# Feed-forward norm weights: from the normalised token rows to the rows of the first feed-forward weights

## The chip, the cores and the metric

One core of a Trainium2 chip. The metric is the device time of one execution of the whole program in microseconds, as the median of several runs. Everything is float32 in and out. The engines are TensorE (PE, with its weight loads as PEld), VectorE (DVE), ScalarE (ACT), GpSimd (POOL), and SyncE (SP), which here only issues transfers. Each engine works through its own list of instructions in order.

## The reference, cut to what matters

A transformer-like block on 1024 tokens of width 1024: two mixing branches, a cross-attention into 256 memory tokens, then a gated feed-forward layer. The part that the change touches is the norm ahead of the feed-forward layer and that layer's first product.

```python
def rms_norm(x, gain):
    y = x * lax.rsqrt(jnp.mean(x * x, axis=-1, keepdims=True) + RMS_EPS)
    return y * gain
...
h = h + memory_cross_attention(rms_norm(h, norm_mem_q), rms_norm(mem, norm_mem_kv), ...)
f_a, f_b = jnp.split(rms_norm(h, norm_ffn) @ w_ffn_in, 2, axis=-1)    # 1024 x 5632
h = h + (jax.nn.silu(f_a) * f_b) @ w_ffn_out
```

`norm_ffn` has one weight for each of the 1024 channels of a token. Since those channels are the inner dimension of the first product, (r · h · diag(g)) @ W equals (r · h) @ (diag(g) · W): the weight may be multiplied into a column of the tokens or into a row of W.

## The kernel before

**Products.** Each float32 matrix product is made from halves: a value is split into a rounded part (hi, written by ScalarE: `split`, "CAST" in the rows) and the rest (lo, a subtraction on VectorE), and three matmuls add hi·hi, hi·lo and lo·hi. On top of that the big products use a seven-product scheme (Strassen's kind) over 2 x 2 blocks. So the weights go through sums and differences before they are split, and the tokens do too (`A11`, `A12`, `S1` to `S4` and `A22` are the seven token operands, each in hi and lo).

**Normalised tokens.** `norm_blocks(t)` handles one tile of 128 tokens, t = 0 to 7, woven between the last rows of the cross-attention (`mem_out`). It takes the root of the mean square (`rstd`: squares on ScalarE into `ss`, a power on GpSimd into `r`, a refinement on VectorE), forms the normalised rows `xs` (in `norm_scale`, one VectorE instruction that multiplies by the root and by a row `gbc` of weights), transposes `xs` on TensorE and builds the token operands. The row of weights comes from `bcast_gain`, a transfer that repeats the 1024 weights on all 128 partitions.

**The first feed-forward weights.** There are 22 hidden tiles of 128 columns (`NF`). For tile j two blocks of 1024 rows x 128 columns are fetched, `raw` (the a half) and `rawb` (the b half), each as 128 partitions x 8 row blocks x 128 columns, 512 KB. `w_first` splits raw into `whi` and `wlo`. `w_sums` makes sums inside raw and rawb on VectorE and splits three of them. `w_last` splits what is left into `wdh` and `wdl`; its second split is the last reader of raw. Tiles 0 and 1 take another way: `ahead` fetches them much earlier as `wpr`, during the gated linear units of the mixing stage, and parks all split operands in a scratch tensor (`w_d`).

**The loop over hidden tiles**, from tile 2 on:

```python
for j in range(2, NF):
    start(j); end(j - 1); w_last(j); middle(j)
    if j + 1 < NF:
        w_first(j + 1); w_sums(j + 1)
    f = w_fetch(j + 2) if j + 2 < NF else f
    if j % 2: out_fetch(j // 2, f.ins)
    else:     gated(j // 2 - 1)
```

`start` runs products 1 and 2 of tile j and copies them out (`a`), `end` runs products 3 and 4 of tile j - 1 and makes the gated result `g` (GpSimd multiplies its second half, a · c), `middle` runs products 6, 7 and 5 (copied out as `a` and `c`). For every second tile `gated` builds four sums of two gated tiles and stores them (`c_d`), and for every other one `out_fetch` loads two row blocks of the second feed-forward weights (`wo`), whose sums `out_sums` puts into `t_d`.

**What sets the order.** A scheduler orders each engine's list and adds the semaphores; tiles come from pools. `raw` has two buffers for all tiles, `rawb` shares five buffers (tag "tmp") with `g` and others, and a transfer into a buffer goes out when the last reader of its former tile is done. PSUM banks are named `mm` (three), `sc` (two), `pv` (two) and `misc`. All fetches of weights stand in SP's one list.

**Around it.** During the cross-attention GpSimd multiplies the attention weights by one over their sum (`pe <- pe,sm`, a column spread over a row), during the gated linear units it multiplies by gates (`sg <- sg,ga`), and earlier, in the mixing attention, it makes low halves (`pl <- pf,ph`). In the second feed-forward product blocks `or` are fetched and split into `oh` and `ol`.

The functions that the change touches, and what calls them:

Of the kernel before, what the change touches and what calls it, by code (L numbers as in the profile page):

```python
# [9 lines left out]
F32 = mybir.dt.float32  # L10
# [3 lines left out]
AF = mybir.ActivationFunctionType  # L14
ALU = mybir.AluOpType
# [4 lines left out]
P = 128  # L20
# [46 lines left out]
def f32(ap):  # L67
    return ap.bitcast(F32)
# [53 lines left out]
class Shared:  # L122
# [5 lines left out]
    def tmp(self, name, dt=F32):  # L128
        return self.pool.tile([P, D], dt, tag="tmp", bufs=5, name=name)
# [15 lines left out]
class Block:  # L145
# [25 lines left out]
    def behind(self, ins):  # L171
        return nullcontext() if ins is None else self.tc.issue_after(ins.ins)

    def wload(self, pieces, cols, pool_lo=False, behind=None, into=None):

        raw = self.wpool.tile([P, RAW], F32, tag="raw", bufs=2, name="raw")
        for off, shape, src in pieces:
            n = shape[0] * shape[1]
            self.S.dma_start(raw[:, off:off + n].rearrange("p (k c) -> p k c", k=shape[0]), src)
        hi, lo = into or [self.wpool.tile([P, WSLOT], F32R, tag=t_, name=t_) for t_ in ("whi", "wlo")]  # L180
        with self.behind(behind):
            self.split(hi[:, :cols], lo[:, :cols], raw[:, :cols], pool_lo)
        return hi, lo

    def wblock(self, w, k0, nk, c0, nc_, pool_lo=False, behind=None):

        src = w[k0 * P:(k0 + nk) * P, c0:c0 + nc_].rearrange("(k p) c -> p k c", p=P)
        hi, lo = self.wload([(0, (nk, nc_), src)], nk * nc_, pool_lo, behind)
        return tuple(t[:, :nk * nc_].rearrange("p (k c) -> p k c", k=nk) for t in (hi, lo))

    def product(self, ps, l, r, start, stop, a=None, **kw):
# [142 lines left out]
def hybrid_block_kernel(ctx: ExitStack, tc: tile.TileContext, x, mem, norm_mix, w_in, b_forget,  # L334
# [36 lines left out]
    with tc.tile_pool(name="st2", bufs=1, reuse_waits="tile") as s2:  # L371
        stage_tail(B, big, s2, sh, x, glu, aT, gate_d, kv_d, sums_d, w_fox_o, w_mix_out, norm_mem_q[0], w_mem_q,
                   w_mem_o, norm_ffn[0], w_ffn_in, w_ffn_out, norm_final, out)
# [226 lines left out]
def stage_tail(B, big, s2, sh, x, glu, aT, gate_d, kv_d, sums_d, w_fox_o, w_mix_out, g_mq, w_mem_q, w_mem_o, g_ffn,  # L600
               w_ffn_in, w_ffn_out, g_fin, out):
    nc, V, A, G, T, S, small, ident = B.nc, B.V, B.A, B.G, B.T, B.S, B.small, B.ident
    NS2 = 16

    def bslot(dt=F32, name="b"):
        return big.tile([P, D], dt, tag="big", name=name)

    def slot(dt=F32, name="t"):
        return s2.tile([P, D], dt, tag="t", bufs=NS2, name=name)
# [6 lines left out]
        return t_  # L616


    am_d = B.dram.tile([4, P, D], F32, name="am_d")
    s3_d = B.dram.tile([2, P, D], F32, name="s3_d")  # L620
    fox, part, xm, mixw, msets = {}, {}, {}, {}, []
# [78 lines left out]
    def ahead(j, mk):  # L700

        def keep(n, t_):
            A.dma_start(w_d[j, n], f32(t_))

        def pair(n):
            hl = mk("wph", F32R), mk("wpl", F32R)
            return hl, [[t_[:, o:o + 512] for t_ in hl] for o in (0, 512)]

        def fetch():
            pre[j] = [mk("wpr") for _ in range(2)]  # L710
            for r_, c in zip(pre[j], (0, FH)):
                S.dma_start(r_.rearrange("p (k c) -> p k c", k=8),
                            w_ffn_in[:, c + j * P:c + (j + 1) * P].rearrange("(k p) c -> p k c", p=P))

        def plain():
            hl, _ = pair(0)
            B.split(*hl, pre[j][0])
            for i, t_ in enumerate(hl):
                keep(i, t_)

        def sums():
            ra, rb = pre[j]
            b22 = rb[:, 512:]
            hl, (w5, w6) = pair(2)
            V.tensor_add(ra[:, 512:], ra[:, 512:], b22)
            V.tensor_add(ra[:, :512], ra[:, :512], rb[:, :512])
            V.tensor_add(rb[:, :512], rb[:, :512], b22)
            B.split(*w5, ra[:, :512])
            V.tensor_add(ra[:, 512:], ra[:, 512:], ra[:, :512])
            V.tensor_add(ra[:, :512], ra[:, :512], b22)  # L730
            B.split(*w6, ra[:, :512])
            for i, t_ in enumerate(hl):
                keep(2 + i, t_)

        def seventh():
            e_ = mk("wph", F32R)
            B.split(e_[:, :512], e_[:, 512:], pre[j][1][:, :512])
            keep(4, e_)

        def rest():  # L740
            ra, rb = pre.pop(j)
            hl, (w3, w4) = pair(5)
            B.split(*w3, rb[:, 512:])
            B.split(*w4, ra[:, 512:])
            for i, t_ in enumerate(hl):
                keep(5 + i, t_)

        return [fetch, plain, sums, seventh, rest]

    ahead0, ahead1 = ahead(0, lambda name, dt=F32: slot(dt, name)), ahead(1, tmp)  # L750
    for j in range(8):
        if j > 3:
# [26 lines left out]
    H = [bslot(name=f"h{t}") for t in range(NT)]  # L779
# [52 lines left out]

    weave([lambda h=h: mem_q(h, 0) for h in range(MH)], [lambda t=t: turned(t, ("misc", "pv")) for t in range(4, 8)])
    kth, ktl, vh, vl = [slot(F32R, "kv") for _ in range(4)]
    gf = B.bcast_gain(s2, g_ffn)
    sc = float(DH * 2) ** -0.5
    pts, oT, pes = {}, {}, {}

# [90 lines left out]
    def put(name, mk, i, src, neg=False):  # L929

        hi_, lo_ = blocks(name, mk)
        for kk in range(2):
            sv = src[:, kk * 256:(kk + 1) * 256].rearrange("p (k c) -> p k c", k=2)
            hi, lo = [a[kk][:, :, i * P:(i + 1) * P] for a in (hi_, lo_)]
            if neg:
                A.activation(hi, sv, AF.Copy, scale=-1.0)
                V.scalar_tensor_tensor(out=lo, in0=sv, scalar=-1.0, in1=f32(hi), op0=ALU.mult, op1=ALU.subtract)
            else:
                B.split(hi, lo, sv)

    def norm_blocks(t):
        i = t % 4
        xs = s2.tile([P, D], F32, tag="xs", bufs=1, name="xs")
        B.norm_scale(xs, H[t], B.rstd(H[t]), gf)
        S.dma_start(h_d[t], H[t])
        ps = [B.turn(xs, b, ("misc", "pv")[b]) for b in range(2)]
        if t < 4:
            for b in range(2):
                xf = sh.half("xf")
                A.copy(xf, ps[b])  # L950
                S.dma_start(x_d[i][:, 512 * b:512 * b + 512], xf)
                put(("A11", "A12")[b], slot, i, xf)
            return
        xa, sx, s3 = tmp("xa"), tmp("sx"), sh.half("s3")
        S.dma_start(xa, x_d[i])
        a11, a12, s1n, a22 = xa[:, :512], xa[:, 512:], sx[:, :512], sx[:, 512:]
        A.copy(a22, ps[1])
        V.tensor_sub(s3, a11, ps[0])
        V.tensor_sub(s1n, ps[0], a22)
        V.tensor_sub(a11, s1n, a11)  # L960
        V.scalar_tensor_tensor(out=a12, in0=a11, scalar=-1.0, in1=a12, op0=ALU.mult, op1=ALU.subtract)
        put("S2", slot, i, a11)
        put("S3", bslot, i, s3)
        put("S1", bslot, i, s1n, neg=True)
        S.dma_start(r_d[i][:, :512], a12)
        S.dma_start(r_d[i][:, 512:], a22)
# [9 lines left out]
    def w_fetch(j):  # L976
        raws[j] = B.wpool.tile([P, RAW], F32, tag="raw", bufs=2, name="raw")[:, :D], tmp("rawb")
        for r_, c in zip(raws[j], (0, FH)):
            f = S.dma_start(r_.rearrange("p (k c) -> p k c", k=8),
                            w_ffn_in[:, c + j * P:c + (j + 1) * P].rearrange("(k p) c -> p k c", p=P))  # L980
        return f

    def wpair(j):
# [136 lines left out]
    for t in range(4):  # L1120
        mem_out(t)
        if t:
            norm_blocks(t - 1)
        for f in late[4 * t:4 * t + 4 if t < 3 else None]:
            f()
    norm_blocks(3)
    w_first(0)
    w_first(1)
    for t in range(4, 8):
        mem_out(t)  # L1130
        if t > 4:
            norm_blocks(t - 1)
    w_sums(0)
    start(0)
    norm_blocks(7)
    start(1)
    w_fetch(2)
    w_last(0)
    w_sums(1)
# [6 lines left out]
    middle(1)  # L1146
    w_sums(2)
    out_fetch(0, w_fetch(3).ins)
    for j in range(2, NF):
        start(j)  # L1150
        end(j - 1)
        w_last(j)
        middle(j)
        if j + 1 < NF:
            w_first(j + 1)
            w_sums(j + 1)
        f = w_fetch(j + 2) if j + 2 < NF else f
        if j % 2:
            out_fetch(j // 2, f.ins)
        else:  # L1160
            gated(j // 2 - 1)
# [66 lines left out]
    for m, (n, p) in enumerate(seq):  # L1228
# [6 lines left out]
        if n < 3 and p in (2, 4, 6, 8):  # L1235
            t = 4 * (n - 1) + p // 2 - 1
# [802 lines left out]
```

## Time and profile before

| | us |
|---|---|
| median of 3 runs (lowest, highest) | 1493.9 (1493.74, 1496.89) |
| the profiled execution, its time | 1489.17 |
| its span, first to last instruction | 1487.5 |
| PE busy | 1447.5 (97%) |
| DVE busy | 1026.5 (69%) |
| ACT busy | 681.6 (46%) |
| POOL busy | 274.2 (18%) |
| mean granted TensorE clock | 0.998 |

Times inside the span count from its first instruction. The cross-attention with the norms lies at about 717 to 910 us, the loop over the first feed-forward weights from there to about 1285 us, the second feed-forward product and the last norm behind it; the gated linear units of the mixing stage, with the `wpr` fetches, lie at about 530 to 715 us.

How its rows read. A group row has a source line, the engine, the operation, output and inputs by the program's names, how often, busy time, the mean of one in ns, and the idle time of the engine just ahead with what ended it. A timeline row has the start, the duration, the engine, line and operation, and in brackets how long the engine had waited and for whom. A row of waits names who waited, for whom, how many us in all, how often, and the longest. SPq is the queue of SyncE, its rows are transfers issued. A duration can hold time in which the instruction stood on its engine without working.

### The profile page before, as it was taken

The numbers are of one execution on the slowest core, as the hardware profiler recorded it, in microseconds if no ns is written. First come the engines' busy times: TensorE is split into PE (matmuls) and PEld (weight loads), VectorE is DVE, ScalarE is ACT, GpSimd is POOL, SyncE is SP. The second block draws the span as 40 slices with busy tenths as digits, with TensorE's granted clock in tenths as the row PEclk, the third lists the DMA queues.
The fourth block names the chain that finished last, engine by engine and source line by source line (L and its number), as shares of the span: only waits on it lengthen the run. The fifth ranks groups of instructions, "written<-read, shape, count | busy, mean of one in ns | idle before, by whom it ended". The sixth has DMA issues, their size and how long they took to land.

```text
span 1487.5 us, 20506 instructions
## 1 busy us (share of the span) xinstructions
PE 1447.5 (97%) x7271; PEld 1248.2 (84%) x7271; DVE 1026.5 (69%) x1841; ACT 681.6 (46%) x1215; POOL 274.2 (18%) x359
## 2 busy tenths in 40 slices
PE   8999999999999999999999999999999999999997
PEld 7889888988777678788888778888888888888886
DVE  7678544555777857689766787777777776576555
ACT  6423333423667764444545654333333333354443
POOL 1036675200112114210102200000000000101001
PEclk9999999999999999999999999999999999999999
DMA  9565668642132476778431376555555554897553
GB/s 303 129 152 117 194 183 151 189 136 35 16 63 54 114 214 204 240 248 316 151 100 57 142 256 233 163 163 163 170 169 166 169 167 159 300 391 256 200 169 114
DMA packets 202249, 257.14 MB, mean 173 GB/s; under 512 B 36041, under 2 KB 127081, under 8 KB 201634
## 3 DMA queue, kind: packets, MB, share of 16 engines
q1 hardware_dynamic: 194946, 239.05, 53.2%
q10 hardware_dynamic: 7200, 16.78, 3.0%
q8 instruction: 57, 0.93, 0.3%
q14 instruction: 46, 0.38, 0.1%
HBM read 175.56 MB, written 83.20 MB: 174 GB/s over the span
## 4 chain that ended last, share of the span: by engine, by line
PE 80%; DVE 8%; DMA 4%; ACT 4%; issue 3%; POOL 1%; SPq 0%; POOLq 0%; DVEq 0%; ACTq 0%
PE mm L196 37%; PE sc L196 16%; PE pv L196 16%; PE mm L142 3%; PE misc L196 2%; PE mm L194 1%; DMA raw<-in_w_mem_kv_dram 1%; DMA or<-in_w_ffn_out_dram 1%; DVE junk L1803 1%; PE sc L194 1%; ACT pf L1835 1%; DVE wlo L213 1%; DVE xs L255 1%; DVE hb L1774 1%; POOL r L231 1%
## 5 line engine op out<-in xcount | busy, mean ns | idle before, releaser
L213 DVE TENSOR_TENSOR wlo<-raw,whi 128x1024 fp32r<-128x1024 f32 (+2 forms) x119 | 128.4, 1082 | 86.8 <-ACT whi L212 83.9
L212 ACT CAST whi<-raw 128x1024 fp32r<-128x1024 f32 (+2 forms) x119 | 107.4, 903 | 131.5 <-DVE raw L1015 29.0
L213 DVE TENSOR_TENSOR ol<-or,oh 128x1024 fp32r<-128x1024 f32 x73 | 92.0, 1266 | 62.2 <-ACT oh L212 61.1
L212 ACT CAST oh<-or 128x1024 fp32r<-128x1024 f32 x73 | 76.4, 1048 | 94.8 <-PE pv L196 30.6
L196 PE MATMUL mm<-uh,whi 128*128 128x512 f32 x280 | 107.6, 384 | 0.1
L196 PE MATMUL mm<-uh,wlo 128*128 128x512 f32 x280 | 106.5, 381 | 0.2 <-DVE wlo L213 0.2
L196 PE MATMUL mm<-ul,whi 128*128 128x512 f32 x280 | 106.3, 380 | 0.0
L1076 POOL TENSOR_TENSOR g<-a,c 128x512 f32<-128x512 f32 x22 | 35.3, 1607 | 363.4 <-ACT a L1075 344.8
L231 POOL TENSOR_TENSOR r<-ms,mhalf 128x1 f32<-128x1 f32 (+1 forms) x30 | 20.5, 686 | 320.0 <-DVE ms L227 252.0
L1838 POOL TENSOR_TENSOR pl<-pf,ph 128x512 fp32r<-128x512 f32 (+1 forms) x32 | 37.3, 1166 | 224.2 <-DVE ph L1837 224.2
L1835 ACT ACTIVATE pf<-sc 128x512 f32<-128x512 f32 (+1 forms) x96 | 46.8, 490 | 35.0 <-DVE sc L1831 21.3
L196 PEld LDWEIGHTS mm<-uh,wlo 128*128 128x128 f32 x280 | 52.9, 189 | 8.4 <-DVE wlo L213 1.3
L196 PEld LDWEIGHTS mm<-uh,whi 128*128 128x128 f32 x280 | 53.1, 190 | 6.3 <-DVE mc L1803 0.4
L196 PEld LDWEIGHTS mm<-ul,whi 128*128 128x128 f32 x280 | 53.1, 190 | 6.0
L196 PE MATMUL pv<-S3h,we 128*128 128x512 f32 x176 | 56.4, 380 | 0.2 <-ACT S3h L212 0.2
L1841 DVE TENSOR_TENSOR pl<-pf,ph 128x512 fp32r<-128x512 f32 (+2 forms) x64 | 34.9, 550 | 17.8 <-ACT ph L1840 17.2
L196 PE MATMUL mm<-yh,whi 128*128 128x512 f32 x104 | 39.5, 383 | 3.9 <-ACT sg L1287 3.4
L1300 POOL TENSOR_TENSOR sg<-sg,ga 128x512 f32<-128x512 f32 x16 | 29.1, 1840 | 72.3 <-DVE sg L1293 27.6
L196 PE MATMUL mm<-oh,ol 128*128 128x512 f32 x106 | 40.2, 379 | 0.0
L196 PE MATMUL mm<-oh 128*128 128x512 f32 x106 | 40.2, 379 | 0.0
L196 PE MATMUL mm<-ol,oh 128*128 128x512 f32 x106 | 40.2, 379 | 0.0
L196 PE MATMUL sc<-uh,whi 128*128 128x512 f32 x104 | 39.8, 383 | 0.0
(722 smaller groups left out, 4609.2 us busy)
## 6 DMA issues: line engine op xcount, KB each, us to landing
or<-c_d SPq DMA_DIRECT2D x77, 256.0 KB
wo<-in_w_ffn_out_dram SPq DMA_DIRECT2D x22, 512.0 KB
c_d<-g SPq DMA_DIRECT2D x44, 256.0 KB
t_d<-wo SPq DMA_DIRECT2D x44, 256.0 KB
or<-t_d SPq DMA_DIRECT2D x44, 256.0 KB
raw<-in_w_ffn_in_dram SPq DMA_DIRECT2D x20, 512.0 KB
rawb<-in_w_ffn_in_dram SPq DMA_DIRECT2D x20, 512.0 KB
raw<-in_w_in_dram SPq DMA_DIRECT2D x18, 512.0 KB
```

What stands on the lines that cost most here:

```text
L142: return lambda *a, **k: self.tc.keep_in_program_order(op(*a, **k))
L194: return self.T.matmul(ps, l, r, start=start, stop=stop)
L196: self.T.matmul(woven(ps, a).rearrange(order), l, halves(r, a).rearrange(order), start=start, stop=stop, **kw)
L212: self.copied = self.A.copy(hi, src)
L213: self.lowered = (self.G if pool_lo else self.V).tensor_sub(lo, src, f32(hi))
L231: self.G.tensor_tensor(out=r, in0=v, in1=self.mhalf[:, 0:n], op=ALU.pow)
L255: self.V.scalar_tensor_tensor(out=xs, in0=src, scalar=r, in1=gb, op0=ALU.mult, op1=ALU.mult)
L1076: G.tensor_mul(g[:, 512:], a1, c1)
L1300: self.B.G.tensor_mul(self.out[j][:, cs], self.out[j][:, cs], ga)
L1835: self.exp = A.activation(halves(pf[:, off:], 64), woven(ps[:, off:], 64), AF.Exp)
L1838: G.tensor_sub(pl[:, off:], pf[:, off:], f32(ph[:, off:]))
L1841: V.tensor_sub(pl[:, off:], pf[:, off:], f32(ph[:, off:]))
```

## The change

It does three things. A new transfer at the program's start loads the 1024 weights as eight columns of 128 (`gain_columns`, tile `gf`), so that row p of row block k finds its weight on its own partition. `row_gain`, one GpSimd instruction over 128 x 1024, multiplies a fetched block of first weights by those columns, in place; it stands behind each fetch of `raw`, `rawb` and `wpr`, 44 times in all. And `norm_blocks` scales the tokens by their root alone, with one ScalarE activation in place of VectorE's instruction. The row of weights `gbc` is not loaded any more.

```diff
+    def gain_columns(self, g, name):
+        gc = self.const.tile([P, 8], F32, name=name)
+        self.S.dma_start(gc, g.rearrange("(k p) -> p k", p=P))
+        return gc
+
+    def row_gain(self, w, gc):
+        wv = w.rearrange("p (k c) -> p k c", k=8)
+        self.G.tensor_tensor(out=wv, in0=wv, in1=gc.unsqueeze(2).to_broadcast([P, 8, wv.shape[-1]]), op=ALU.mult)
...
+    gf = B.gain_columns(g_ffn, "gf")
     am_d = B.dram.tile([4, P, D], F32, name="am_d")
...
             for r_, c in zip(pre[j], (0, FH)):
                 S.dma_start(r_.rearrange("p (k c) -> p k c", k=8),
                             w_ffn_in[:, c + j * P:c + (j + 1) * P].rearrange("(k p) c -> p k c", p=P))
+                B.row_gain(r_, gf)
...
-    gf = B.bcast_gain(s2, g_ffn)
...
         xs = s2.tile([P, D], F32, tag="xs", bufs=1, name="xs")
-        B.norm_scale(xs, H[t], B.rstd(H[t]), gf)
+        A.activation(xs, H[t], AF.Copy, scale=B.rstd(H[t]))
         S.dma_start(h_d[t], H[t])
...
             f = S.dma_start(r_.rearrange("p (k c) -> p k c", k=8),
                             w_ffn_in[:, c + j * P:c + (j + 1) * P].rearrange("(k p) c -> p k c", p=P))
+            B.row_gain(r_, gf)
         return f
```

`wload` and `wblock` also get a parameter `gain` that no caller sets. Lines of the changed file lie 10 to 13 further down than those of before (L1076 is now L1089, L858 is L870, L212 is L223).

**Three places in the order of instructions.** GpSimd's list at the start of the loop, before (`r` is the root of a norm, `g` the gated half):

```order
L231 TENSOR_TENSOR r_8944<-ms_8943,mhalf 128x1
L231 TENSOR_TENSOR r_9027<-ms_9026,mhalf 128x1
L1076 TENSOR_TENSOR g<-a_9174,c_9200 128x512
L1076 TENSOR_TENSOR g<-a_9253,c_9279 128x512
L1076 TENSOR_TENSOR g<-a_9386,c_9412 128x512
```

The same place after:

```order
L242 TENSOR_TENSOR r_9031<-ms_9030,mhalf 128x1
L181 TENSOR_TENSOR rawb<-rawb,gf 128x1024 x2
L1089 TENSOR_TENSOR g<-a_9180,c_9206 128x512
L181 TENSOR_TENSOR rawb<-rawb,gf 128x1024
L1089 TENSOR_TENSOR g<-a_9259,c_9285 128x512
L181 TENSOR_TENSOR raw<-raw,gf 128x1024
L181 TENSOR_TENSOR rawb<-rawb,gf 128x1024
L1089 TENSOR_TENSOR g<-a_9394,c_9420 128x512
```

Between two products g of the loop now stand one product of raw and one of rawb; g itself waits behind them in GpSimd's list.

GpSimd's list in the cross-attention, before:

```order
L231 TENSOR_TENSOR r_7578<-ms_7577,mhalf 128x1
L858 TENSOR_TENSOR pe<-pe,sm 128x512 x11
L231 TENSOR_TENSOR r_8315<-ms_8314,mhalf 128x1
L231 TENSOR_TENSOR r_8439<-ms_8438,mhalf 128x1
L858 TENSOR_TENSOR pe<-pe,sm 128x512 x2
```

And after:

```order
L870 TENSOR_TENSOR pe<-pe,sm 128x512 x5
L181 TENSOR_TENSOR raw<-raw,gf 128x1024
L870 TENSOR_TENSOR pe<-pe,sm 128x512 x2
L181 TENSOR_TENSOR raw<-raw,gf 128x1024
L870 TENSOR_TENSOR pe<-pe,sm 128x512 x4
L242 TENSOR_TENSOR r_8319<-ms_8318,mhalf 128x1
```

The products of the first two raw tiles (2 and 3) stand in the midst of the attention weights' products.

VectorE's list at the norm of the last token tile, before:

```order
L237 TENSOR_TENSOR rt_9028<-r_9027 128x1
L238 SCALAR_TENSOR_TENSOR rt_9028<-rt_9028,ms_9026 128x1
L239 SCALAR_TENSOR_TENSOR r_9027<-rt_9028,r_9027 128x1
L255 SCALAR_TENSOR_TENSOR xs<-h_6956,r_9027,gbc 128x1024
L958 TENSOR_TENSOR s_9048<-xa,misc 128x512
```

After, VectorE's list, where the row of xs is gone:

```order
L248 TENSOR_TENSOR rt_9032<-r_9031 128x1
L249 SCALAR_TENSOR_TENSOR rt_9032<-rt_9032,ms_9030 128x1
L250 SCALAR_TENSOR_TENSOR r_9031<-rt_9032,r_9031 128x1
L970 TENSOR_TENSOR s_9052<-xa,misc 128x512
L1064 TENSOR_TENSOR a_9010<-a_9010,sc 128x512
```

And ScalarE's list after, where it has come in:

```order
L223 CAST S2h<-xa 128x2x128 x2
L1065 ACT_TABLE_LOAD
L1065 ACTIVATE a_9010<-a_9010 128x512
L956 ACTIVATE xs<-h_6960,r_9031 128x1024
L223 CAST whi<-raw 128x1024
L1062 COPY a_9087<-mm 128x512
```

The scaling stands behind a Silu of `start(0)` and ahead of the cast of a raw tile and the copy of a bank.

More of the change, by code (lines that the diff above doesn't have):

```diff
@@ L172, in behind, with wload @@
         return nullcontext() if ins is None else self.tc.issue_after(ins.ins)
-    def wload(self, pieces, cols, pool_lo=False, behind=None, into=None):
+    def gain_columns(self, g, name):
[5 more added lines that the diff above has]
+        self.G.tensor_tensor(out=wv, in0=wv, in1=gc.unsqueeze(2).to_broadcast([P, 8, wv.shape[-1]]), op=ALU.mult)
+    def wload(self, pieces, cols, pool_lo=False, behind=None, into=None, gain=None):
         raw = self.wpool.tile([P, RAW], F32, tag="raw", bufs=2, name="raw")
@@ L180, in wload @@
         hi, lo = into or [self.wpool.tile([P, WSLOT], F32R, tag=t_, name=t_) for t_ in ("whi", "wlo")]
+        if gain is not None:
+            self.row_gain(raw[:, :cols], gain)
         with self.behind(behind):
@@ L183, in wload, with wblock @@
         return hi, lo
-    def wblock(self, w, k0, nk, c0, nc_, pool_lo=False, behind=None):
+    def wblock(self, w, k0, nk, c0, nc_, pool_lo=False, behind=None, gain=None):
         src = w[k0 * P:(k0 + nk) * P, c0:c0 + nc_].rearrange("(k p) c -> p k c", p=P)
-        hi, lo = self.wload([(0, (nk, nc_), src)], nk * nc_, pool_lo, behind)
+        hi, lo = self.wload([(0, (nk, nc_), src)], nk * nc_, pool_lo, behind, gain=gain)
         return tuple(t[:, :nk * nc_].rearrange("p (k c) -> p k c", k=nk) for t in (hi, lo))
```

## The prediction

> **What bounds the kernel now.** I read the page first: its span and section 1.
>
> ```profile
> span 1487.5 us, 20506 instructions
> PE 1447.5 (97%) x7271; PEld 1248.2 (84%) x7271; DVE 1026.5 (69%) x1841; ACT 681.6 (46%) x1215; POOL 274.2 (18%) x359
> ```
>
> TensorE bounds it: it idles for 40 us in all, and GpSimd (POOL) looks free. But a share says nothing of a stage, so next come the stretches with the changed work: cross-attention with the norms (800 to 910 us), and the loop over the first feed-forward weights. Each row of this table has a stretch, its length, and then what PE, PEld, DVE, ACT and POOL are busy in it.
>
> ```profile
> 800.00:910.00 110.00, 103.32 (x538) 86.12 (x537) 87.11 (x199) 64.04 (x178) 15.34 (x18) 1.00 0.54 192
> 910.00:1255.00 345.00, 345.00 (x1600) 302.11 (x1600) 256.81 (x361) 132.00 (x210) 31.55 (x20) 1.00 0.51 164
> ```
>
> In the loop TensorE never idles, and its clock is full (1.00). What could make it idle is seen from the waits of the engines that feed it.
>
> ```profile
> DVE wlo L213 <- ACT whi L212: 51.0, 24, 3.2
> DVE wdl L213 <- PE pv L196: 14.1, 11, 1.7
> DVE g L1071 <- PE mm L196: 7.8, 8, 1.1
> ACT whi L212 <- DMA raw<-in_w_ffn_in_dram: 25.3, 11, 3.4
> ```
>
> VectorE (DVE) waits longest for a cast on ScalarE (ACT), and that waits for the weight's transfer. So I followed one raw tile through two tiles of the loop, in timelines by engine.
>
> ```profile
> 1001.76 1.22 DVE L213 TENSOR_TENSOR wlo<-raw,whi 128x1024 fp32r<-128x1024 f32 x1 [2.77 <-ACT whi L212]
> 1014.21 0.68 DVE L213 TENSOR_TENSOR wdl<-raw,wdh 128x512 fp32r<-128x512 f32 x1
> 1014.43 1.60 POOL L1076 TENSOR_TENSOR g<-a,c 128x512 f32<-128x512 f32 x1 [16.60 <-ACT a L1075]
> 1014.81 1.77 DVE L1115 TENSOR_TENSOR wo<-wo 128x512 f32<-128x512 f32 x1
> 1014.92 0.38 SPq L979 DMA_DIRECT2D raw<-in_w_ffn_in_dram  x1
> 1018.88 1.04 ACT L212 CAST whi<-raw 128x1024 fp32r<-128x1024 f32 x1
> 1019.96 1.23 DVE L213 TENSOR_TENSOR wlo<-raw,whi 128x1024 fp32r<-128x1024 f32 x1 [2.78 <-ACT whi L212]
> 1020.32 0.59 ACT L1063 COPY c<-mm 128x512 f32<-128x512 f32 x1 [0.39 <-PE mm L196]
> 1028.09 0.69 DVE L1071 SCALAR_TENSOR_TENSOR g<-mm,a 128x512 f32<-128x512 f32 x1 [1.07 <-PE mm L196]
> 1030.46 0.69 DVE L213 TENSOR_TENSOR wdl<-rawb,wdh 128x512 fp32r<-128x512 f32 x1 [1.69 <-PE pv L196]
> 1032.27 0.68 DVE L213 TENSOR_TENSOR wdl<-raw,wdh 128x512 fp32r<-128x512 f32 x1
> 1033.03 0.38 SPq L979 DMA_DIRECT2D raw<-in_w_ffn_in_dram  x1
> 1037.93 1.22 DVE L213 TENSOR_TENSOR wlo<-raw,whi 128x1024 fp32r<-128x1024 f32 x1 [2.69 <-ACT whi L212]
> ```
>
> This is a ring. The last subtraction that reads a raw tile (wdl<-raw, ends 1014.89) frees one of two raw buffers; the fetch goes out at 1014.92; the cast follows at 1018.88; wlo at 1019.96; VectorE, in order, works to the next wdl<-raw (ends 1032.95); then the next fetch. Its four legs: 1001.76 to 1014.89, 13.1 us, with the four sums of `gated`; 5.1 to 1019.96; 13.0 to 1032.95, of which 1.07 + 1.69 = 2.8 us are waits for TensorE; 5.0 to 1037.93. Without those waits the ring needs 33.4 us for two tiles, and TensorE takes 36.2. So the ring is slack by 2.8 us, no more.
>
> A second thing stands there. POOL's product begins at 1014.43 and VectorE's 128x512 addition takes 1.77 us instead of 0.68: it is held until POOL ends (1016.03). The other way, a VectorE operation that reads PSUM is not held while POOL works:
>
> ```profile
> 607.88 2.50 POOL L1300 TENSOR_TENSOR sg<-sg,ga 128x512 f32<-128x512 f32 x2 [10.44 <-DMA ga<-gate_d]
> 609.76 0.69 DVE L647 TENSOR_TENSOR gb<-gb,pv 128x512 f32<-128x512 f32 x1 [3.84 <-DMA gb<-gate_d]
> ```
>
> **The change, part by part.** *44 products of 128x1024 on POOL.* The trace has no such size; the nearest rows are half of it.
>
> ```profile
> L858 POOL TENSOR_TENSOR pe<-pe,sm 128x512 f32<-128x512 f32 x16 | 16.6, 1040 | 60.1 <-DVE sm L856 59.8
> L1838 POOL TENSOR_TENSOR pl<-pf,ph 128x512 fp32r<-128x512 f32 x24 | 30.6, 1276 | 69.3 <-DVE ph L1837 69.3
> L1076 POOL TENSOR_TENSOR g<-a,c 128x512 f32<-128x512 f32 x22 | 35.3, 1607 | 363.4 <-ACT a L1075 344.8
> ```
>
> The first also spreads a column over a row, as the new product does: 2 x 1.04 = 2.1 us, which I take. Twice the second, 2.55, and twice the third (which holds waits behind VectorE), 3.2, are the upper ends. By the Trainium skill's GPSIMD Engine Reference, section 3.1, a float32 tensor_tensor of 2048 elements takes 4497 ns on this engine; half of it is an estimate of 2.25 us, and the sum below would rise from 34 to about 39 us with it. No run here shows that size yet.
>
> *In the loop* the product of raw stands between the landing and the cast: twice 2.1 per two tiles on the two short legs. 33.4 + 4.2 = 37.6 us, 1.4 over TensorE's 36.2. The products of rawb hold VectorE while it works on the long legs:
>
> ```profile
> 1008.35 0.39 SPq L979 DMA_DIRECT2D rawb<-in_w_ffn_in_dram  x1
> 1019.90 0.43 SPq L979 DMA_DIRECT2D rawb<-in_w_ffn_in_dram  x1
> ```
>
> The first comes 6.6 us after its leg begins and needs four to land, so it is multiplied before that leg's wdl<-raw; the second comes behind the two wo fetches of the leg before and lands within the next leg. Each holds 2.1 less one PSUM operation of 0.6 that passes: 1.5. Together 40.6, so 4.4 us more than TensorE needs. Low end: no hold, 1.4. High end: 2.55 instead of 2.1 in all four (1.8), nothing passes (1.2), and POOL's g comes before wdl<-raw instead of behind it (1.1): 8.5.
>
> The Trainium skill (SBUF — State Buffer, "Who interferes with whom") says that a VectorE instruction with two SBUF inputs and a GpSimd instruction that reads SBUF exclude each other for a whole instruction, and one with a single SBUF input is free. The 1.77 and the 0.69 us above agree; by a shared bandwidth instead, the ring would take the 37.6 us.
>
> How TensorE is reached: the copy c (1020.32, 0.59 us) is queued on ScalarE behind the raw cast, and the third product into that bank needs it, at this row of the chain:
>
> ```profile
> 1025.46 2.59 PE mm L196 x12
> ```
>
> The cast ends at 1019.92 and could end at 1025.46 - 0.59 = 1024.87: a head start of 4.9 us. Raw fetches run every 18.1 us from 924.24 to 1232.69:
>
> ```profile
> 924.24 0.38 SPq L979 DMA_DIRECT2D raw<-in_w_ffn_in_dram  x1
> 1232.69 0.38 SPq L979 DMA_DIRECT2D raw<-in_w_ffn_in_dram  x1
> ```
>
> That is 17 intervals, 8.5 pairs: 8.5 x 4.4 - 4.9 = 32.5 us (low 8.5 x 1.4 - 4.9 = 7, high 8.5 x 8.5 - 4.9 = 67).
>
> *Eight normalisations move from DVE to ACT.* What TensorE waits for them is small, whatever DVE saves:
>
> ```profile
> PE misc L261 <- DVE xs L255: 2.7, 4, 1.5
> L255 DVE SCALAR_TENSOR_TENSOR xs<-h,r,gbc x16: 1275/1284/1287, 717.4 to 886.2; 128x1024 f32<-128x1024 f32 x16
> ```
>
> On ACT one costs about the 1.04 us of the 128x1024 cast, in a stage where ACT is busy for 64 of 110 us. I take a gain of 2.5; the ends are 0 and all idle time of that stage, 110 - 103.3 = 6.7.
>
> *Two products in the cross-attention* stand in POOL's queue ahead of pe products, and POOL waits there for the raw tile:
>
> ```profile
> 804.10 0.38 SPq L979 DMA_DIRECT2D raw<-in_w_ffn_in_dram  x1
> ```
>
> Landing 3.9 us later like those of the loop, it lets the next pe, and TensorE's transposes of it, come up to 1.5 us late: 1.0 taken, 0 to 1.5. The first two rawb products delay the sums of tile 2: 1.0 taken, 0 to 2.
>
> *Four wpr products.* For the first two VectorE has no gap, and TensorE already stalls at the end of that stretch:
>
> ```profile
> 582.79 4.07 POOL L1300 TENSOR_TENSOR sg<-sg,ga 128x512 f32<-128x512 f32 x2 [1.04 <-DVE sg L1293]
> 585.69 1.71 DVE L725 TENSOR_TENSOR wpr<-wpr 128x512 f32<-128x512 f32 x1
> 612.88 0.48 PE L196 MATMUL mm<-yh,whi 128*128 128x512 f32 x1 [3.42 <-ACT sg L1287]
> ```
>
> Two holds of 2.1 are 4.2 us; I take 2.5 at that stall, 0 to 4.2. ACT's cast of wpr waits with them, and the copies behind it evacuate TensorE's banks. The other two fall into POOL's longest rest, ahead of the roots of the next norm:
>
> ```profile
> 716.21 0.57 POOL L231 TENSOR_TENSOR r<-ms,mhalf 128x1 f32<-128x1 f32 x1 [63.20 <-DVE ms L227]
> ```
>
> 0 taken, up to 2 if VectorE, which they hold, gives nothing back before 716.
>
> *The column of weights*, 1024 elements of 4 bytes on SP between the first stage's weights and kv_d: 0. Behind it in the queue are the stores of kv_d and the first gates' weights, which TensorE's input projections cover; no row prices it, so I allow 0 to 2. The row load that goes has nobody waiting.
>
> Sum: 32.5 - 2.5 + 1 + 1 + 2.5 = 34.5 us. The profiled execution took 1489.2 us (span 1487.5), so 1523.7 there. The median of the runs is 1493.9, 0.3% higher; against that 1528.
>
> **The rivals.** (1) *POOL's products do not hold VectorE*: only the latency of the ring counts, +7 +2, 1503. For it: once VectorE ran on unheld and POOL was the one that waited, 6.39 us for two products that took 2.50 above. Against it: the 1.77 us at g.
>
> ```profile
> 591.05 6.39 POOL L1300 TENSOR_TENSOR sg<-sg,ga 128x512 f32<-128x512 f32 x2 [4.19 <-DVE sg L1293]
> 592.08 1.22 DVE L213 TENSOR_TENSOR wlo<-raw,whi 128x1024 fp32r<-128x1024 f32 x1
> ```
>
>  (2) *The ring keeps its slack, and the kernel gets faster*: products hidden, nothing held, and only VectorE's freed time in the norm stage counts: between the 2.7 us of waits for xs and all 6.7 of idle time, 4 off, 1490. That needs less than 2.8 us added per two tiles, so a product of raw under 1.4 us with no hold, or work for VectorE during the wait; the order of the change leaves the sums of `gated` behind wlo, so it has none. (3) *Added and slack are equal*, 2.8 to 3.4 us for two tiles: no change, 1492 to 1496. (4) *Each product takes its turn as g does*, 3.2 us: 33.4 + 4 x 3.2 = 46.2, ten over, 8.5 x 10 - 4.9 + 2 = 82 at most; with one rawb product where VectorE waits anyway 55: 1549 to 1576.
>
> **Chances.** The forecast, 1508 to 1550: 0.63. Rival 1, 1497 to 1508: 0.13. Rival 4: 0.10. Rival 3: 0.08; rival 2: 0.06. The range 1498 to 1553 leaves out rivals 2 and 3 and most of 4, two in ten. Slower by over 0.2% (what a measurement of this kernel can tell, 3 us) has the first three, 0.86; faster 0.06, same 0.08.
>
> **What would show it.** Right: in the loop raw fetches every 20 us instead of 18.1; TensorE waiting for the copy c of L1063 (after), some 2 us per tile; casts of raw ended by POOL; products of raw near 2.1 us and VectorE operations of 2 to 3 us beside those of rawb; DVE xs gone from TensorE's waits. Wrong: a fetch interval still at 18.1, or raw products under 1.4 us; an interval of 20 us with TensorE waiting for VectorE's sums instead would leave the number and refute the place.

## The result, and the profile after

The changed kernel takes 1550.8 us, median of 6 runs (1543.4 to 1554.0), against 1494.3 us: 1.0377 times as long, interval 1.036 to 1.0394, so 56.5 us more. The forecast was 1528 with a range of 1498 to 1553. The direction came out, and the ring as the mechanism. The time lies 2 us inside the range and just outside the band of 1508 to 1550 that had most of the chances, and the place at which TensorE waits is another than the one forecast.

The first lines of the page of the changed kernel, and its chain of waits by engine:

```profile
span 1549.9 us, 20518 instructions
PE 1468.6 (95%) x7271; PEld 1258.0 (81%) x7271; DVE 1049.5 (68%) x1833; ACT 684.4 (44%) x1223; POOL 359.6 (23%) x403
PE 49%; DVE 20%; DMA 13%; ACT 8%; issue 4%; POOL 3%; SPq 1%; POOLq 0%; DVEq 0%; ACTq 0%
```

GpSimd is still busy for less than a quarter of the time, and yet the chain that ends last is TensorE's for half of it, where it was 80% before. Now the same stretch as before, the loop, in the changed kernel: first its busy times (PE, PEld, DVE, ACT, POOL), then who waited for whom in it.

```profile
942.00:1297.00 355.00, 324.88 (x1443) 277.36 (x1442) 254.26 (x326) 113.27 (x189) 95.90 (x52) 0.97 0.44 145
ACT whi L223 <- POOL raw L181: 101.5, 17, 7.7
POOL raw L181 <- DMA raw<-in_w_ffn_in_dram: 58.9, 17, 5.1
ACT a L1088 <- DVE a L1087: 34.4, 17, 3.2
PEld mm L207 <- ACT a L1072: 28.6, 13, 4.2
PE mm L207 <- ACT a L1072: 23.6, 12, 3.8
PE mm L207 <- ACT c L1076: 6.5, 5, 2.2
```

TensorE, which never idled here, now idles for 30 of 355 us. The loop is some 46 us longer than before; the other 16 are busy time, 325 us where the kernel before has 309 from 924 to 1233 us, at a mean clock of 0.97 (the row's eighth column) instead of 1.00; the last section has the slow matmuls. The casts of raw wait for GpSimd's product, 17 times, and the product for the transfer. One turn of the ring, put together from the timelines of the engines (start, duration, engine):

```profile
1067.90 0.38 SPq L991 DMA_DIRECT2D raw<-in_w_ffn_in_dram  x1
1071.99 1.90 POOL L181 TENSOR_TENSOR raw<-raw,gf 128x1024 f32<-128x1024 f32 x1 [3.04 <-DMA raw<-in_w_ffn_in_dram]
1073.92 1.05 ACT L223 CAST whi<-raw 128x1024 fp32r<-128x1024 f32 x1 [6.17 <-POOL raw L181]
1075.00 1.23 DVE L224 TENSOR_TENSOR wlo<-raw,whi 128x1024 fp32r<-128x1024 f32 x1 [4.90 <-ACT whi L223]
1085.64 1.90 POOL L181 TENSOR_TENSOR rawb<-rawb,gf 128x1024 f32<-128x1024 f32 x1 [11.75 <-DMA rawb<-in_w_ffn_in_dram]
1085.68 2.40 DVE L224 TENSOR_TENSOR wdl<-rawb,wdh 128x512 fp32r<-128x512 f32 x1
1088.00 0.68 DVE L1087 TENSOR_TENSOR a<-a,pv 128x512 f32<-128x512 f32 x1
1088.71 0.63 ACT L1088 ACTIVATE a<-a 128x512 f32<-128x512 f32 x1 [3.15 <-DVE a L1087]
1089.20 0.68 DVE L224 TENSOR_TENSOR wdl<-raw,wdh 128x512 fp32r<-128x512 f32 x1
1089.25 0.57 ACT L1072 COPY a<-mm 128x512 f32<-128x512 f32 x1
1089.87 0.48 PE L207 MATMUL mm<-S1h,whi 128*128 128x512 f32 x1 [3.67 <-ACT a L1072]
1089.96 0.38 SPq L991 DMA_DIRECT2D raw<-in_w_ffn_in_dram  x1
1095.05 1.90 POOL L181 TENSOR_TENSOR raw<-raw,gf 128x1024 f32<-128x1024 f32 x1 [4.02 <-DMA raw<-in_w_ffn_in_dram]
1098.06 1.23 DVE L224 TENSOR_TENSOR wlo<-raw,whi 128x1024 fp32r<-128x1024 f32 x1 [5.88 <-ACT whi L223]
1109.91 0.38 SPq L991 DMA_DIRECT2D raw<-in_w_ffn_in_dram  x1
```

The fetch of a raw tile goes out when wdl<-raw has ended; the product, the cast and wlo follow; then VectorE works in order to the next wdl<-raw. In this turn the product of rawb at 1085.64 starts 0.04 us ahead of wdl<-rawb, which stands for 2.40 us instead of 0.68. Behind it on VectorE is the sum a, behind that on ScalarE the Silu, and behind that the copy of a bank for which TensorE has waited 3.67 us.

### The profile page after: what moved, and what is told of

The parts are those of the page before. It is cut to its first block, busy times and chain, and to the rows that moved or that the text cites. A ratio compares the mean times of both kernels' runs of the same rounds, so it can differ in the third digit from the quotient of the medians.

```text
span 1549.9 us, 20518 instructions
## 1 busy us (share of the span) xinstructions
PE 1468.6 (95%) x7271; PEld 1258.0 (81%) x7271; DVE 1049.5 (68%) x1833; ACT 684.4 (44%) x1223; POOL 359.6 (23%) x403
## 4 chain that ended last, share of the span: by engine, by line
PE 49%; DVE 20%; DMA 13%; ACT 8%; issue 4%; POOL 3%; SPq 1%; POOLq 0%; DVEq 0%; ACTq 0%
PE mm L207 22%; PE sc L207 12%; PE pv L207 8%; DMA raw<-in_w_ffn_in_dram 4%; PE mm L142 3%; DVE wlo L224 3%; ACT whi L223 2%; DVE wdl L224 2%; POOL raw L181 2%; DMA raw<-in_w_in_dram 2%; DVE wo L1128 1%; PE misc L207 1%; DMA c_d<-s 1%; DMA raw<-in_w_mem_kv_dram 1%; DMA or<-in_w_ffn_out_dram 1%
## 5 line engine op out<-in xcount | busy, mean ns | idle before, releaser
L223 ACT CAST whi<-raw 128x1024 fp32r<-128x1024 f32 (+2 forms) x119 | 107.5, 904 | 243.5 <-POOL raw L181 107.3
L223 ACT CAST oh<-or 128x1024 fp32r<-128x1024 f32 x73 | 76.4, 1048 | 93.3 <-PE mm L207 31.8
L1851 POOL TENSOR_TENSOR pl<-pf,ph 128x512 fp32r<-128x512 f32 (+1 forms) x32 | 37.3, 1167 | 229.3 <-DVE ph L1850 147.2
L181 POOL TENSOR_TENSOR rawb<-rawb,gf 128x1024 f32<-128x1024 f32 x20 | 43.7, 2183 | 171.3 <-DMA rawb<-in_w_ffn_in_dram 131.2
L207 PE MATMUL mm<-S1h,whi 128*128 128x512 f32 x88 | 38.2, 434 | 23.6 <-ACT a L1072 23.6
L1089 POOL TENSOR_TENSOR g<-a,c 128x512 f32<-128x512 f32 x22 | 35.5, 1612 | 101.0 <-ACT a L1088 101.0
L207 PE MATMUL pv<-S3h,we 128*128 128x512 f32 x176 | 56.5, 380 | 0.0
L181 POOL TENSOR_TENSOR raw<-raw,gf 128x1024 f32<-128x1024 f32 x20 | 37.9, 1897 | 74.7 <-DMA raw<-in_w_ffn_in_dram 68.1
L207 PEld LDWEIGHTS mm<-S1h,whi 128*128 128x128 f32 x88 | 18.6, 211 | 31.6 <-ACT a L1072 28.9
L207 PE MATMUL mm<-S4h,wdh 128*128 128x512 f32 x88 | 34.2, 388 | 8.6 <-ACT c L1076 6.8
L1313 POOL TENSOR_TENSOR sg<-sg,ga 128x512 f32<-128x512 f32 x16 | 24.6, 1559 | 75.0 <-DMA ga<-gate_d 33.5
```

Source lines behind the costliest of these rows:

```text
L181: self.G.tensor_tensor(out=wv, in0=wv, in1=gc.unsqueeze(2).to_broadcast([P, 8, wv.shape[-1]]), op=ALU.mult)
L207: self.T.matmul(woven(ps, a).rearrange(order), l, halves(r, a).rearrange(order), start=start, stop=stop, **kw)
L223: self.copied = self.A.copy(hi, src)
L1089: G.tensor_mul(g[:, 512:], a1, c1)
L1313: self.B.G.tensor_mul(self.out[j][:, cs], self.out[j][:, cs], ga)
L1851: G.tensor_sub(pl[:, off:], pf[:, off:], f32(ph[:, off:]))
```

## Where the time went, place by place

The lists of instructions are nearly the same in all kernels, so one may take the same ScalarE instruction in two traces and subtract its starts. The table gives this delay against the trace of before, in us, at five places (by their time before): the mixing stage ahead of the first wpr product (573) and behind it (598), the start of cross-attention (732), the first copy c (900) and the last (1274). What the kernels are is said below.

| kernel | 573 | 598 | 732 | 900 | 1274 |
|---|---|---|---|---|---|
| changed | 5.9 | 10.5 | 12.9 | 16.9 | 62.3 |
| e_noprod | 2.4 | 2.4 | 3.2 | 2.9 | 3.8 |
| e_wpr | 1.7 | 6.7 | 12.0 | 10.0 | 11.0 |
| e_raw | 4.7 | 7.9 | 12.9 | 14.9 | 29.6 |
| e_rawb | 1.5 | 5.0 | 8.7 | 10.3 | 16.8 |
| e_last | 5.5 | 8.6 | 12.1 | 16.9 | 17.9 |
| e_raw4 | 1.8 | 4.9 | 9.0 | 12.4 | 14.8 |
| e_loop | 6.3 | 6.3 | 11.8 | 11.1 | 12.0 |

Up to 573 no kernel differs but for the load of the weight column, and that column is there in kernels with 1.5 as with 6.3, so nothing here can be put down to the change. The trace of before is one of its short ones (1489.2 us against a median of 1494), so every other trace starts with a debt of some microseconds. What the change costs is the growth between columns: in the changed kernel 7.0 in the mixing stage, 4.0 in cross-attention with the norms, 45.4 in the loop. A growth of some microseconds in one trace proves nothing by itself, though: e_loop has no wpr product and still grows by 5.5 between 598 and 732, for which no cause was found. Only what several traces show together is read below.

## The experiments

**Only the scaling on ScalarE (e_noprod).** No column, no products:

```diff
-    gf = B.gain_columns(g_ffn, "gf")
...
-                B.row_gain(r_, gf)
...
-            B.row_gain(r_, gf)
```

> The token rows are scaled by their root on ScalarE, and nothing else of the change is there: no column of weights, no product on GpSimd; the feed-forward norm weights are left out of the result. My theory of the norm stage (VectorE's eight scalings gone, ScalarE's in their place, worth 0 to 6.7 us, taken as 2.5) gives 1487 to 1494, likeliest 1491. Rival: ScalarE's place for the scaling, behind other work in its list, makes TensorE wait for xs longer than VectorE did; then 1494 to 1500, and the stretch of the norms is longer than before. The delay of 5.5 us that the changed kernel's trace has at 290 to 355 us, far ahead of any product, is absent if the column of weights causes it, and can be there if it is a whim of the transfers.

Measured 1494.1 us (1490.1 to 1497.3) against 1493.7, ratio 1.0002 (0.9987 to 1.0018). The trace gains 0.3 from 732 to 900, and 2.0 from 757 on, where the norms begin; the runs show nothing. So the work taken off VectorE is worth nothing that can be measured, and no cheaper way of multiplying the weight rows could have made this change a gain of more than the 2 us that the interval leaves open.

**The wpr products alone (e_wpr).** As the change, without the products in the loop's fetches:

```diff
-            B.row_gain(r_, gf)
         return f
```

> The column of weights, the ScalarE scaling and the four products of wpr are in; the 40 products of raw and rawb are left out, so those weight rows are unscaled. Ring theory: the loop's fetch interval is back at 18.1 us and the time is that of the outside terms alone. By the changed kernel's trace these are 0.6 (start) + 5.5 (290 to 355 us) + 6.8 (mixing stage) and the norm stage: 1500 to 1509. If the trace's 5.5 us is not from the change, 1497 to 1503. Rival: what slows the loop is not the products but the ScalarE scaling and the shifted order; then the loop stays slow and the time over 1530.

Measured 1500.7 us (1496.9 to 1502.7), ratio 1.0039 (1.0026 to 1.0052): 5.8 us for four products. The loop is at its old pace (10.0 at its first copy c, 11.0 at its last), which refutes the rival: ScalarE's scaling and the shifted order do the loop no harm.

**One of the two products in the loop.** First raw's alone (e_raw), then rawb's alone (e_rawb, `if c:`):

```diff
-            B.row_gain(r_, gf)
+            if c == 0:
+                B.row_gain(r_, gf)
```

> The changed kernel without its 20 products of rawb (those rows are unscaled); the products of raw stay. Ring theory: short legs of 7.1 and 7.5 us as in the changed kernel, long legs without a held instruction 13.2 and 10.2: 38.0 us for two tiles against 36.3 before, so 1.7 x 8.5 = 15 us in the loop, 12 to 16 outside: 1520 to 1526. Rival, the products of rawb alone do the harm by holding VectorE, whose late sum delays the Silu and the copy of a bank behind it: loop nearly at 18.1 us again, 1506 to 1512.

> The changed kernel without its 20 products of raw (those rows are unscaled); the products of rawb stay. Ring theory: short legs 5.0 and 5.1 us, long legs 15.2 and 11.6 as in the changed kernel: 37.0 us for two tiles against 36.3, so 6 us in the loop, 12 to 16 outside: 1512 to 1517. Rival, the holds reach TensorE directly by the late sum, Silu and copy a, whatever the ring does: its waits for copy a of 3.7 us per two tiles stay, 3.7 x 8.5 = 31 us in the loop, 1535 to 1542.

Measured 1518.9 us (ratio 1.016, 1.0138 to 1.0182) with raw's alone and 1511.1 us (1.0106, 1.0066 to 1.0145) with rawb's alone, both about 1 us under what the ring theory said. SyncE's timelines have the first and the last fetch of raw in the loop, 17 intervals apart, of the changed kernel, of the one with raw's products and of the one with rawb's:

```profile
942.12 0.38 SPq L991 DMA_DIRECT2D raw<-in_w_ffn_in_dram  x1
1296.83 0.38 SPq L991 DMA_DIRECT2D raw<-in_w_ffn_in_dram  x1
```

```profile
940.12 0.38 SPq L991 DMA_DIRECT2D raw<-in_w_ffn_in_dram  x1
1264.63 0.38 SPq L991 DMA_DIRECT2D raw<-in_w_ffn_in_dram  x1
```

```profile
936.85 0.38 SPq L991 DMA_DIRECT2D raw<-in_w_ffn_in_dram  x1
1253.75 0.38 SPq L991 DMA_DIRECT2D raw<-in_w_ffn_in_dram  x1
```

Divided by 8.5, that is 41.7, 38.2 and 37.3 us for two tiles, against 36.3 before: 5.4 more with both products, 1.9 and 1.0 with one of them. (Long and short intervals alternate, and 17 of them hold nine long ones; the last 16 alone give 41.5, 38.0 and 37.0.) Both together cost 2.6 more than the sum of the two. That is what a ring with a slack of 2.8 us does: each product alone has the slack to itself, together they have it once. The rival in which the holds reach TensorE without the ring would have had the larger part with rawb's products; it has the smaller, and TensorE's matmuls wait for the copy a 1.2 us in all in that kernel's loop, where the rival had 31.

**The last reader of raw goes first (e_last).** The whole change, and two lines of `w_last` exchanged:

```diff
         ra, rb = raws.pop(j)
-        B.split(*wts[j, 3], rb[:, 512:])
         B.split(*wts[j, 4], ra[:, 512:])
+        B.split(*wts[j, 3], rb[:, 512:])
```

> The whole change, and in w_last the two splits in the other order: the last reader of raw comes first, so that the raw buffer is free earlier. Ring theory: in VectorE's list wdl<-raw now stands ahead of the sum a, a wo sum and wdl<-rawb, so each fetch goes out 1.8 us earlier, and 1.7 us more where wdl<-rawb is the held instruction: 36.2 (TensorE's own) to 37.8 us for two tiles instead of 41.5. With 12 us outside the loop that is 1506 to 1520, and the waits of TensorE for copy a shrink with it. Rival: the copy a comes late because of the held VectorE instructions themselves and not because the ring is late; then those waits stay and the time is over 1535.

Measured 1504.0 us (1500.4 to 1506.9), ratio 1.0064 (1.0044 to 1.0083): of 56 us some 46 are gone, with all 44 products in place. The loop of this kernel, in the same columns as above, and its first and last fetch of raw:

```profile
940.00:1267.00 327.00, 327.00 (x1517) 286.35 (x1516) 278.33 (x344) 121.89 (x199) 100.92 (x53) 1.00 0.50 166
```

```profile
940.38 0.38 SPq L991 DMA_DIRECT2D raw<-in_w_ffn_in_dram  x1
1248.54 0.38 SPq L991 DMA_DIRECT2D raw<-in_w_ffn_in_dram  x1
```

TensorE is busy for the whole stretch and the interval is 18.1 us again. VectorE's instructions are held as before (wdl<-rawb still has a mean of 1.23 us here), but they now stand behind the instruction that frees the buffer:

```profile
1120.84 0.69 DVE L224 TENSOR_TENSOR wdl<-raw,wdh 128x512 fp32r<-128x512 f32 x1 [0.43 <-PE pv L207]
1121.45 0.68 DVE L1087 TENSOR_TENSOR a<-a,pv 128x512 f32<-128x512 f32 x1
1121.69 0.38 SPq L991 DMA_DIRECT2D raw<-in_w_ffn_in_dram  x1
1122.65 0.69 DVE L224 TENSOR_TENSOR wdl<-rawb,wdh 128x512 fp32r<-128x512 f32 x1
```

VectorE waits for TensorE there again, as in the kernel before. The waits for copy a are gone. That alone does not refute the rival, under which they come from the held instructions and not from the ring: the exchange also takes the sum a out from behind the held wdl<-rawb. The next run leaves it there.

**Four raw buffers (e_raw4).** The whole change, with two tiles that are idle from tile 4 on as further buffers; and the same in the kernel before as a control (e_bef4):

```diff
-        raws[j] = B.wpool.tile([P, RAW], F32, tag="raw", bufs=2, name="raw")[:, :D], tmp("rawb")
+        if j >= 4 and j % 4 < 2:
+            r = s2.tile([P, D], F32, tag=("w1h", "w1l")[j % 4], bufs=1, name="raw")
+        else:
+            r = B.wpool.tile([P, RAW], F32, tag="raw", bufs=2, name="raw")[:, :D]
+        raws[j] = r, tmp("rawb")
```

> The whole change with four raw buffers in the loop instead of two (the other two are tiles that hold tile 1's operands and are idle from tile 4 on). Ring theory: a raw tile lands and is multiplied a tile ahead of its cast, so neither the landing nor the product stands between a fetch and the next; the interval goes back to TensorE's 18.1 us although all 40 products and their holds are there: 12 us outside the loop, 1504 to 1511. Rival: GpSimd's holds on VectorE alone bound the loop; then the interval stays over 19 us and the time is over 1520.

> The kernel before with the same four raw buffers, as a control. Its ring has 2.8 us of slack for two tiles and TensorE does not idle in the loop: 1491 to 1497, no change. If it became faster by more than 3 us, the gain of the four buffers in the changed kernel would be partly one that has nothing to do with the products.

Measured 1504.1 us (1503.8 to 1507.7), ratio 1.0069 (1.0044 to 1.0094), and for the control 1494.1 us, ratio 0.9998 (0.9978 to 1.0018). The loop of the kernel with four buffers, in the same columns:

```profile
940.00:1240.00 300.00, 300.00 (x1392) 262.70 (x1391) 260.98 (x319) 111.67 (x181) 92.39 (x49) 1.00 0.51 167
```

TensorE never idles, although the sum a stands behind wdl<-rawb as in the changed kernel and wdl<-rawb is held (mean 1.23 us). This refutes the rival. A second way out of the ring gives the same time as the first, and neither the buffers nor (next) the exchange gives the kernel before anything.

**What the remaining 10 us are.** The exchange with the products of the first four hidden tiles left out (wpr, and raw and rawb of tiles 2 and 3; e_loop), the first two wpr products alone (e_wpr0), and the exchange in the kernel before (e_beflast):

```diff
             f = S.dma_start(...)
-            B.row_gain(r_, gf)
+            if j >= 4:
+                B.row_gain(r_, gf)
```

> As in the run with the two splits of w_last exchanged, but the products of the first four hidden tiles (the four of wpr, and raw and rawb of tiles 2 and 3) are left out, so those weight rows are unscaled; 36 products in the loop stay. Ring theory: with the exchange all 36 hide, the norm stage has ScalarE's scaling alone (as without any product): 1490 to 1497, likeliest 1494, so that the 10 us that the exchange leaves are those eight products. Rival: part of the 10 us is in the loop (first fetches, holds) or from the exchange; then 1498 to 1504.

> The products of the first two wpr blocks alone (the other 42 are left out), with the column of weights and the ScalarE scaling. By the traces with all four wpr products the first two delay the mixing stage by 3.2 to 5.0 us and the other two by 2.0 to 2.7: 1496 to 1500, likeliest 1498. If the first two cost nothing here: 1494.

> The kernel before with the two splits of w_last exchanged, as a control. The ring only gains slack that TensorE does not use: 1491 to 1497. If it is faster by over 3 us, part of what the exchange gave the changed kernel has nothing to do with the products.

Measured 1495.3 us (ratio 1.0008, 0.9989 to 1.0027), 1498.3 us (1.0035, 1.0023 to 1.0047) and 1493.3 us (0.9994, 0.9983 to 1.0006). So with the exchange 36 products in the loop cost nothing that can be measured, and some 8 of the 10 us are the other eight products. The first two of wpr alone cost 5.2 us by the ratio and four cost 5.8; the runs do not tell these two apart. Rows of GpSimd's and ScalarE's timelines in the changed kernel, and TensorE's waits around them:

```profile
583.17 4.21 POOL L1313 TENSOR_TENSOR sg<-sg,ga 128x512 f32<-128x512 f32 x2 [3.40 <-DVE sg L1306]
587.35 5.22 POOL L181 TENSOR_TENSOR wpr<-wpr,gf 128x1024 f32<-128x1024 f32 x2
590.00 1.05 ACT L223 CAST wph<-wpr 128x1024 fp32r<-128x1024 f32 x1 [5.21 <-POOL wpr L181]
597.06 0.62 ACT L223 CAST wph<-wpr 128x512 fp32r<-128x512 f32 x1 [6.00 <-DVE wpr L739]
597.58 0.59 ACT L1305 ACTIVATE sb<-sc 128x512 f32<-128x512 f32 x1
PE pv L207 <- DVE gb L659: 3.8, 1, 3.8
PE mm L207 <- ACT sg L1300: 1.6, 1, 1.6
```

The products stand behind two gate products, with VectorE busy beside them, and take 5.22 us for two. ScalarE's first cast waits 5.21 us for them. The 6.00 us ahead of its next cast are no cost by themselves: the kernel before has 6.82 us of idle time at that place. TensorE feels the delay at two places, a bank that VectorE's gb<-gb,pv has to free and the evacuation sg<-mm on ScalarE. In the seven kernels that have these two products its matmuls wait there for 5.4 to 7.0 us together, in those without for 2.9 to 4.5; the matmuls' wait for gb is found in those seven alone.

**The product on the token rows instead (e_xpool).** The kernel before with the root applied on ScalarE and the row of weights on GpSimd, eight products in place of 44:

```diff
-        B.norm_scale(xs, H[t], B.rstd(H[t]), gf)
+        B.norm_scale(xs, H[t], B.rstd(H[t]), gf, pool=True)
```

> The kernel before with the norm weights still on the token rows, but in two steps: ScalarE scales by the root, GpSimd multiplies the 128x1024 rows by the row of weights. Eight products on GpSimd in place of 44. VectorE is freed as in the change, xs comes one product of 1.9 us later per tile. If TensorE has other work meanwhile, 1490 to 1496; if every tile's delay reaches TensorE, 8 x 1.9 = 15 us, 1507. Likeliest 1497, since before TensorE waited for xs only 2.7 us in all.

Measured 1501.3 us (1497.9 to 1508.1), ratio 1.0056 (1.0036 to 1.0077), worse than the likeliest value of its expectation. The product and TensorE's wait for it, by the tile xs:

```profile
L253 POOL TENSOR_TENSOR xs<-xs,gbc x8: 2340/2352/2382, 823.0 to 894.1; 128x1024 f32<-128x1024 f32 x8
  POOL xs L253: 22.5, 10
```

Matmuls and weight loads, which overlap, wait 22.5 us in all for GpSimd's xs, the matmuls alone 9.4; by the runs the kernel is 7.5 us longer, some 0.9 of the 2.35 us of each of eight products.

## Why the prediction was right, and where its terms were off

The ring of raw transfers bounds the loop, as forecast. The terms that were off (the longer leg of the ring, the head start, the products outside the loop and the gain in the norms) all made the forecast too small and nothing made up for them; the range held by 2 us.

**The ring: right.** The four legs, means over the loop, forecast and measured: from fetch to wlo 7.2 and 7.1; to the next wdl<-raw, with the sums of `gated`, 14.6 and 15.2; second fetch to wlo 7.1 and 7.5; to wdl<-raw 11.7 and 11.6. The sum is 41.5 instead of 40.6. The holds were priced 1.5 each; the longer leg shows 2.1 and the other 1.4, though in the turn shown above one held instruction stands 1.7 us too long in each (2.40 and, on a sum in raw at 1101.73, 2.39 instead of 0.68). What makes the rest of the difference is not shown. The second landing is slower by 0.4 us.

**The price of a product: right for raw.** Groups of the changed kernel by tile (least, median, most in ns):

```profile
L181 POOL TENSOR_TENSOR raw<-raw,gf x20: 1895/1897/1899, 810.7 to 1301.6; 128x1024 f32<-128x1024 f32 x20
L181 POOL TENSOR_TENSOR rawb<-rawb,gf x20: 1896/2094/3622, 908.8 to 1292.4; 128x1024 f32<-128x1024 f32 x20
L181 POOL TENSOR_TENSOR wpr<-wpr,gf x4: 1898/2494/2639, 587.4 to 679.2; 128x1024 f32<-128x1024 f32 x4
```

1.90 us undisturbed, for which 2.1 was taken. The time of 1550.8 lies in the band of rival 4 (1549 to 1576), but not for its reason: it needed 3.2 us for each product. Rival 1, without holds, falls with the 2.40 us of wdl<-rawb and with the run that has rawb's products alone, whose fetches fall behind by 8 us in the loop.

**The head start: the term that failed in the loop.** Of the ring's surplus, 4.9 us were taken off, because the copy c had that much time to spare. TensorE is reached elsewhere. The sum a on VectorE, the Silu and the copy a form a second path from VectorE's late work to TensorE, and the kernel before shows its spare time (a row of waits, the copy a on ScalarE, and the product that needs it):

```profile
ACT a L1059 <- PE mm L196: 16.5, 20, 0.9
1015.14 0.59 ACT L1059 COPY a<-mm 128x512 f32<-128x512 f32 x1 [0.78 <-PE mm L196]
1017.53 0.38 PE L196 MATMUL mm<-S1h,whi 128*128 128x512 f32 x1
```

ScalarE stood idle for some 0.8 us ahead of each copy a until TensorE had filled the bank. It was free from 1014.36 on, and the copy could have ended as late as 1017.53: 1017.53 - 0.59 - 1014.36 = 2.6 us to spare, about half of what copy c had. Little of it came into play in the loop. Against the kernel before, the first of the fetches above is 17.9 us late and the last 64.1; the copies c are late by 16.9 and 62.3 (table). So TensorE was spared 1.8 us in all, 1.0 of them at the start, and the loop costs it nearly the whole surplus, 45.4 us of 17 x (20.87 - 18.14) = 46, where 32.5 was said. Of the difference some 9 are the ring's longer period and some 4 the head start. The statement that TensorE would wait for copy c is wrong for the larger part: 6.5 and 8.5 us (matmuls and weight loads, which overlap) fall on c, 23.6 and 28.6 on a. The prediction had named a wait for VectorE's sums as what would refute the place; this wait is for a copy behind such a sum, so the place falls.

**The mixing stage: too low.** 2.5 (0 to 4.2) was taken for the first two wpr products; the traces that have them grow by 3.1 to 5.0 there, those without by at most 1.2. For the other two 0 (to 2) was taken; around them, from 654 to 680, the traces with the products grow by 1.9 to 2.7 and those without by at most 0.9. The cause named, ScalarE's casts and the evacuations behind them, is a part of what the rows above show: the cast does wait for the product, but the wait that the products bring to TensorE anew is for VectorE's gb.

**The norms: the gain was too large, the costs beside it too small.** From 757 us, where the norms of cross-attention end and VectorE's scalings were, to the first copy c four kernels have the scaling on ScalarE and no raw or rawb product yet: e_noprod and e_wpr gain 2.0 us in their traces, e_loop 0.7 and e_wpr0 nothing; 2.5 was said. With raw's products alone the same stretch costs 2.0, with rawb's 1.6, with both 4.0 in the changed kernel, 3.5 in e_last and 1.9 in e_raw4. Counted from a gain of 0 to 2.0 that is 1.6 to 4.0 for either and 1.9 to 6.0 for both, where 1.0 and 1.0 had been taken. The part of TensorE's waits for xs, in the stretch from 757 to 910 us before and after, is no smaller:

```profile
L261 PE MATMUL misc<-ident,xs 128*128 128x128 f32 x44 | 6.8, 276 | 2.8 <-DVE xs L255 2.7
```

```profile
L272 PE MATMUL misc<-ident,xs 128*128 128x128 f32 x48 | 7.6, 280 | 3.9 <-ACT xs L956 3.9
```

It was 2.7 for VectorE and is 3.9 for ScalarE.

**The column: right**, no place shows it (573 in the table). All in all the forecast for the change is 34.5 and the runs say 56.5: about 13 of the 22 us too little lie in the loop, the rest outside it, in eight products that were taken as nearly hidden and in a gain of 2.5 that the run without products (1494.1 us) does not show.

## What to carry to other kernels

An engine that is 18% busy is not free: what counts is whether its new work stands between a transfer and the buffer's release, or holds an instruction that does, so measure that ring leg by leg, with the waits taken out, against the engine that bounds. If a ring is slack by 2.8 us, two additions that are harmless or cheap alone can cost much more together, and here the cheapest cure was to move the last reader of the buffer forward in its engine's list (two lines exchanged, 46 us). When a delay is followed to the engine that bounds, look at every path that leaves the late engine and take the one with the least spare time: from when the next engine is free to when its result is needed, less its own work.

## What the runs showed of the hardware that was not expected

After a pause TensorE came back at half its clock in some turns and at full clock in others. The changed kernel, one window behind each of two pauses (the eighth column is the granted clock), and the matmul that ends the first pause (that of the second stands in the turn of the ring above):

```profile
1006.50:1013.00 6.50, 6.20 (x15) 4.93 (x16) 2.59 (x3) 1.29 (x3) 3.26 (x2) 0.50 0.79 239
1089.80:1095.00 5.20, 5.13 (x24) 4.51 (x25) 2.38 (x3) 1.06 (x3) 1.23 (x1) 1.00 0.76 238
1006.80 0.80 PE L207 MATMUL mm<-S1h,whi 128*128 128x512 f32 x1 [3.76 <-ACT a L1072]
```

The pauses had 3.76 and 3.67 us. The Trainium skill (TensorE: Matmul & The Clock Gate, Part 1) says that the clock is halved after a window of some 3.4 us without work, and that this window runs freely; that pauses of nearly the same length end either way agrees with it. By this trace the slow matmuls cost the ring little: VectorE waits in the loop for ScalarE's casts alone (wlo, 99.0 us) and never for TensorE.

The product with a spread column took 1.90 us and the one of the same shape with two full operands (xs<-xs,gbc above) 2.35. From the Trainium skill's figure (GPSIMD Engine Reference, section 3.1) the prediction had estimated 2.25 us; the two groups come out on either side of it, and what sets their instructions apart is the second operand.
